# Product ends by eight k tiles and token halves, and two modulation rows moved beside the indexer, in a two-block transformer kernel

## The chip, the core and the metric

The kernel runs on one core of a Trainium2 chip. The metric is the time of one execution on the device in microseconds. The engines named below are TensorE (PE, matrix products), VectorE (DVE), ScalarE (ACT), GpSimd (POOL) and SyncE (SP), which only issues loads here.

## What is computed

256 tokens of width 1024 go through two transformer blocks of different make, all in float32. Cut to the products and the modulation:

```python
# block 1
h = h + rms_norm(nsa_gmlp_mixer(rms_norm(h)) @ w_out)          # w_out 1024x1024
gate, up = split(rms_norm(h) @ w_gate_up)                      # 1024 x 2*2816
h = h + rms_norm((silu(gate) * up) @ w_down)                   # 2816x1024
# block 2
mod = (silu(c) @ ada_w + ada_b)                                # 1024 x 6*1024
shift_m, scale_m, gate_m, shift_f, scale_f, gate_f = split(mod)   # rows 0 to 5
h = rmsnorm(x) * (1 + scale_m) + shift_m
q_lat, kv_lat, k_idx, w_idx, z, xbc, dt_raw, g_a, g_b = split(h @ w_in)
y_a = sparse_mla_attention(...)    # indexer scores -> top 64 keys -> attention
y_b = ssd_mixer(z, xbc, dt_raw, ...)
x = x + gate_m * rmsnorm((sigmoid(g_a) * (y_a @ w_o_attn) + sigmoid(g_b) * (y_b @ w_o_ssd)) @ w_out)
h2 = rmsnorm(x) * (1 + scale_f) + shift_f
u_gate, u_up = split(h2 @ w_ffn_in)
x = x + gate_f * rmsnorm((silu(u_gate) * u_up) @ w_ffn_out)
```

## The kernel before

**Products.** The 256 tokens are two halves t of 128. Every float32 operand is held as two parts, hi and lo, and a product is three matmuls: hi x hi, lo x hi, hi x lo (`mm3`, L285 to L287; L362 to L364 in `projT`, which makes the transposed result with 256 columns). Weights come in raw tiles of 512 KB that SP loads (`wload`, L268) into NRAW = 6 buffers; ACT copies each to hi (L277) and DVE subtracts to get lo (L278), into NHI = 4 pairs. A raw buffer is free again when its lo is made, a pair when its last matmul has read it.

**proj2** makes a product with 1024 output columns: four k tiles at a time, first half t = 0, then t = 1, two PSUM tiles of 512 columns each (named ma for t = 0 and mb for t = 1). When a half is done, `residual` takes it through a norm, adds it to x, norms again, transposes (`transpose_split`, PE tile tr, L256) and splits the result to xT, which the next product reads. DVE's steps of this chain are L374 to L394, the split of the transposes L245.

**ffn** takes the gate columns 0 to 511 for both halves (PSUM ma), then the up columns (mb), then the remaining columns, then w_down by proj2.

**Work woven in.** `weave` takes steps of two generators by given costs (SCHED). Beside the first feed-forward run `adas` and `key_bias`. `adas((2, 4, 3))` makes three rows of mod: for each row eight loads araw with own buffers, eight accumulations on DVE (L575 the first, L577 the others), and a sum over partitions by four matmuls on 32 columns at a time (L583). `key_bias` has eight steps: a load rb (L683), issued one step ahead into two buffers, two DVE instructions (L696, L697), 48 matmuls (L703), copies by ACT (L705), and four stores of 1 MB (kb) from ACT's queue. Row 5 is made beside the second feed-forward. Rows 1 and 0 are made by a third form, `adas_pe` (L544), before the stages treated here.

**The indexer stage.** `indexer()` makes qi, then for each t eight idx steps: four matmuls (L1210) into a PSUM tile, ACT's Relu (L1213), two DVE accumulations (L1219); then the top-k of the half (L1229, L1230). `weave` sets it beside zproj (the last z columns, `projT`), `steps` (softplus and running sums, L1109 to L1126), four products `gproj` and ssd_in. Engines work through their instructions in the order in which the program issues them, so this order is the schedule.

## Time and profile before

| | us |
|---|---|
| median of 3 runs (lowest, highest) | 1005.57 (999.85, 1005.75) |
| profiled execution | 1006.56 |
| its span, first to last instruction | 1004.8 |
| PE busy | 938.7 (93%) |
| DVE busy | 719.2 (72%) |
| ACT busy | 509.0 (51%) |
| POOL busy | 35.9 (4%) |

200.01 MB are moved, 199 GB/s on the mean; TensorE's mean granted clock is 0.969 of full speed. PE counts as busy when a matmul is under way, also a slow one. The stages are, in the span's microseconds: w_out to 175.2, the first feed-forward to about 392, the indexer stage from about 418 to 580, w_out_2 782 to 807, the second feed-forward to 1002.

### The profile page before, as it was taken

Reading aid. Unit: us, or ns where it says so; the run is one execution under the profiler, and the core shown is the slowest. Engines: PE = TensorE matmul, PEld = TensorE weight load, DVE = VectorE, ACT = ScalarE, POOL = GpSimd, SP = SyncE. Lnnn points to the kernel's source line nnn. Section 1 sums busy time; section 2 is a strip of 40 time slices with the busy share of each in tenths; the row PEclk is TensorE's granted clock in tenths of the full one; section 3 lists DMA queues with packets and bytes.
Section 4 is the critical chain, followed back from the end, with each engine's and each line's share of the span. In section 5 each row is a group of like instructions: output and inputs, shape, how many; then the busy total and the mean of one; then the engine's idle time right before and its main releaser. Section 6 shows DMA issues by size and latency. Waiting matters only on the chain.

```text
span 1004.8 us, 16187 instructions
## 1 busy us (share of the span) xinstructions
PE 938.7 (93%) x6161; PEld 790.0 (79%) x6161; DVE 719.2 (72%) x1305; ACT 509.0 (51%) x873; POOL 35.9 (4%) x63
## 2 busy tenths in 40 slices
PE   8879988899999997899799999999999979999997
PEld 6755656689998775797688789899867859999885
DVE  5754864697978577579988657899876677776544
ACT  5333634453445335465557656867753454544432
POOL 2000001000000001100000000000000010000000
PEclk9997998999999999899989999999999999999999
DMA  9775557888899894565444179677665668766651
GB/s 296 210 250 205 169 168 205 256 222 273 224 300 288 271 299 123 136 179 160 147 128 152 57 225 235 168 176 205 179 178 169 208 180 269 233 199 182 226 171 42
DMA packets 157115, 200.01 MB, mean 199 GB/s; under 512 B 14868, under 2 KB 118317, under 8 KB 157037
## 3 DMA queue, kind: packets, MB, share of 16 engines
q1 hardware_dynamic: 137840, 184.61, 61.6%
q10 hardware_dynamic: 16268, 8.30, 3.0%
q0 software_dynamic: 2928, 6.07, 2.0%
q8 instruction: 48, 0.79, 0.3%
q14 instruction: 31, 0.25, 0.1%
HBM read 193.39 MB, written 5.54 MB: 198 GB/s over the span
## 4 chain that ended last, share of the span: by engine, by line
PE 68%; DMA 13%; DVE 10%; issue 3%; ACT 3%; POOL 1%; SPq 0%; ACTq 0%; DVEq 0%; POOLq 0%
PE ma L286 7%; PE ma L287 7%; PE ma L285 7%; DMA raw<-in_w_gate_up_dram 5%; PE ma L362 4%; PE ma L364 4%; PE ma L363 4%; PE mb L286 4%; PE mb L287 4%; PE mb L285 4%; PE mb L362 4%; PE mb L363 3%; PE mb L364 3%; DVE lo L278 3%; DMA rb<-t 2%
## 5 line engine op out<-in xcount | busy, mean ns | idle before, releaser
L278 DVE TENSOR_TENSOR lo<-raw,hi 128x1024 fp32r<-128x1024 f32 (+2 forms) x266 | 320.7, 1213 | 133.5 <-ACT hi L277 129.2
L277 ACT CAST hi<-raw 128x1024 fp32r<-128x1024 f32 (+2 forms) x266 | 275.4, 1044 | 255.4 <-PE mb L287 78.8
L364 PE MATMUL ma<-xTh,lo 128*128 128x256 f32 x512 | 144.7, 283 | 6.8 <-DVE lo L278 6.8
L362 PE MATMUL ma<-xTh,hi 128*128 128x256 f32 x512 | 146.5, 286 | 1.0 <-ACT hi L277 1.0
L363 PE MATMUL ma<-xTl,hi 128*128 128x256 f32 x512 | 144.3, 282 | 0.0
L362 PE MATMUL mb<-xTh,hi 128*128 128x256 f32 x384 | 106.9, 278 | 0.0
L363 PE MATMUL mb<-xTl,hi 128*128 128x256 f32 x384 | 106.6, 278 | 0.0
L364 PE MATMUL mb<-xTh,lo 128*128 128x256 f32 x384 | 106.5, 277 | 0.0
L364 PEld LDWEIGHTS ma<-xTh,lo 128*128 128x128 f32 x512 | 98.3, 192 | 8.0 <-DVE lo L278 7.6
L362 PEld LDWEIGHTS ma<-xTh,hi 128*128 128x128 f32 x512 | 98.3, 192 | 4.1 <-issue 2.5
L363 PEld LDWEIGHTS ma<-xTl,hi 128*128 128x128 f32 x512 | 98.2, 192 | 1.0 <-issue 0.8
L286 PE MATMUL ma<-lo,xTh 128*128 128x512 f32 (+2 forms) x208 | 84.4, 407 | 11.3 <-DVE lo L278 11.3
L285 PE MATMUL ma<-hi,xTh 128*128 128x512 f32 (+2 forms) x208 | 84.2, 408 | 0.1
L287 PE MATMUL ma<-hi,xTl 128*128 128x512 f32 (+2 forms) x208 | 83.8, 403 | 0.2
L362 PEld LDWEIGHTS mb<-xTh,hi 128*128 128x128 f32 x384 | 72.2, 188 | 1.2 <-issue 1.2
L363 PEld LDWEIGHTS mb<-xTl,hi 128*128 128x128 f32 x384 | 72.2, 188 | 0.8 <-issue 0.8
L364 PEld LDWEIGHTS mb<-xTh,lo 128*128 128x128 f32 x384 | 72.2, 188 | 0.6 <-DVE lo L278 0.4
L286 PEld LDWEIGHTS ma<-lo,xTh 128*128 128x128 f32 x208 | 41.3, 198 | 22.4 <-DVE lo L278 14.3
L285 PEld LDWEIGHTS ma<-hi,xTh 128*128 128x128 f32 x208 | 40.7, 197 | 12.0 <-issue 2.9
L287 PEld LDWEIGHTS ma<-hi,xTl 128*128 128x128 f32 x208 | 41.0, 197 | 9.1 <-DVE xTl L245 1.1
L286 PE MATMUL ma<-lo,hTh 128*128 128x512 f32 x88 | 35.4, 402 | 4.4 <-DVE lo L278 4.4
L577 DVE SCALAR_TENSOR_TENSOR ada<-araw,t,ada 128x1024 f32<-128x1024 f32 x28 | 35.8, 1279 | 5.0 <-DMA araw<-in_ada_w_dram 5.0
(431 smaller groups left out, 1805.2 us busy)
## 6 DMA issues: line engine op xcount, KB each, us to landing
raw<-in_w_in_dram SPq DMA_DIRECT2D x80, 512.0 KB, 4.7
raw<-in_w_gate_up_dram SPq DMA_DIRECT2D x44, 512.0 KB, 11.7
raw<-in_w_ffn_in_dram SPq DMA_DIRECT2D x44, 512.0 KB, 4.7
araw<-in_ada_w_dram SPq DMA_DIRECT2D x32, 512.0 KB, 5.6
raw<-in_w_down_dram SPq DMA_DIRECT2D x22, 512.0 KB, 10.7
raw<-in_w_ffn_out_dram SPq DMA_DIRECT2D x22, 512.0 KB, 3.5
raw<-in_w_out_dram SPq DMA_DIRECT2D x16, 512.0 KB, 4.4
cw<-in_ada_w_dram SPq DMA_DIRECT2D x16, 512.0 KB, 4.0
```

The costliest lines, as they stand in the source:

```text
L277: s.copy(hi, raw)
L278: v.tensor_tensor(lo, raw, hi.bitcast(F32), op=OP.subtract)
L285: pe.matmul(out, xh, wh, start=start, stop=False)
L286: pe.matmul(out, xh, wl, start=False, stop=False)
L287: pe.matmul(out, xl, wh, start=False, stop=stop)
L362: pe.matmul(out, hi[:, k % pc, fs], xh[:, k], start=k == 0, stop=False)
L363: pe.matmul(out, hi[:, k % pc, fs], xl[:, k], start=False, stop=False)
L364: pe.matmul(out, lo[:, k % pc, fs], xh[:, k], start=False, stop=k == KT - 1)
L577: v.scalar_tensor_tensor(acc, raw, cc, acc, op0=OP.mult, op1=OP.add)
```

## The change

It has three parts. (1) For w_out and w_out_2 `proj2` takes `tail=8`: the last group has all eight k tiles (w_down and w_ffn_out keep four), so that t = 0 is done with 48 matmuls of t = 1 still to come. Of the eight, the first four go k tile by k tile, the last four by column half. Four more pairs hx and lx (pool tx) are used in turn with hi and lo, from the product to the first four steps of the feed-forward behind it. (2) The feed-forward's first gate and up products are taken in turn by half: gate and up of t = 0, then of t = 1; four steps of this are taken before `weave` starts. (3) Rows 4 and 3 leave `adas`; `ada_fill` makes them in steps driven by the indexer: 16 loads into the common raw buffers, and for each 128x1024 tile four matmuls (L607 after) that sum over k in PSUM, with one DVE addition a row. `key_bias` goes ahead of `adas` in their mix.

```diff
-SCHED = {"a1": (2.0, 1.08), "f1": (3.0, 3.8), "f1ada": (2, 4, 3), "a2": (2.0, 0.63), "f2": (3.0, 1.45),
+SCHED = {"a1": (2.0, 1.08), "f1": (3.0, 3.1), "f1ada": (2,), "a2": (2.0, 0.63), "f2": (3.0, 1.45),
...
+    def deeper(side=None):
+        with pool("tx", side="right") as tx:
+            deep[:] = [tx, -1]
...
     def wsplit(raw, shape):
         n = int(np.prod(shape))
-        hi = T(wp, [P, CH], F32R, tag="hi", bufs=NHI)[:, :n].rearrange("p (a n) -> p a n", a=shape[0])
-        lo = T(wp, [P, CH], F32R, tag="lo", bufs=NHI)[:, :n].rearrange("p (a n) -> p a n", a=shape[0])
+        pl, tags, bufs = wp, ("hi", "lo"), NHI
+        if deep:
+            deep[1] = (deep[1] + 1) % (NHI + NTX)
+            if deep[1] >= NHI:
+                pl, tags, bufs = deep[0], ("hx", "lx"), NTX
+        hi, lo = (T(pl, [P, CH], F32R, tag=z, bufs=bufs)[:, :n].rearrange("p (a n) -> p a n", a=shape[0])
+                  for z in tags)
...
-                for ci, c in [(ci, c) for c in range(2) for ci in grp] if last else [(ci, c) for ci in grp for c in range(2)]:
+                cut = max(0, len(grp) - 4) if last else len(grp)
+                for ci, c in [(ci, c) for ci in grp[:cut] for c in range(2)] + [(ci, c) for c in range(2)
+                                                                               for ci in grp[cut:]]:
...
-            yield from proj(w_up, 0, 512, 8, xT, keep, sizes=(4,))
-            yield from proj(w_up, DFF, 512, 8, xT, finish(0, 512), sizes=(4,), bank=mb)
+            yield from mix(proj(w_up, 0, 512, 8, xT, keep, sizes=(4,)),
+                           proj(w_up, DFF, 512, 8, xT, finish(0, 512), sizes=(4,), bank=mb))
...
+    def ada_fill(js):
...
+                raws[i] = wload(ktile(I["ada_w_2"], k, 1, j * D, D), (1, 1024))[:, 0]
+        load(0)
+        load(1)
+        yield
+        for i, (j, k) in enumerate(todo):
+            raw = raws.pop(i)
+            if k == 0:
+                b = mb()[:, :256]
+            for c in range(4):
+                pe.matmul(b[c * 32:(c + 1) * 32], c32[:, k], raw[:, c * 256:(c + 1) * 256], start=k == 0, stop=k == 7)
+            load(i + 2)
+            if k == 7:
+                q = qs[j]
+                v.tensor_tensor(q[:, 0], b, q[:, 0], op=OP.add)
+                mod_store(j, q[:, 0], q[:, 1] if j in gains else None)
+            yield
...
-        run(proj2(I["w_out"][0], 8, mT, ev_o, order=[4, 5, 6, 7, 0, 1, 2, 3]))
+        run(proj2(I["w_out"][0], 8, mT, ev_o, order=[4, 5, 6, 7, 0, 1, 2, 3], tail=8))
...
-    weave((ffn(xT, I["w_gate_up"][0], I["w_down"][0], rf, ev_f1), wa),
-          (mix(adas(SCHED["f1ada"], rp), key_bias()), wd))
+    with pool("rp", side="right") as rp:
+        weave((f1g, wa), (mix(key_bias(), adas(SCHED["f1ada"], rp)), wd))
...
-    weave((seq(indexer(), latent_v(), heads()), wa), (seq(zproj(NZ0, NZ - NZ0), once(steps, srow), *gproj, ssd_in(0, ap)), wf))
+    weave((seq(indexer(ada_fill((4, 3))), latent_v(), heads()), wa),
+          (seq(zproj(NZ0, NZ - NZ0), once(steps, srow), *gproj, ssd_in(0, ap)), wf))
...
-    shift = mod_row(3, sp, "E0", 2)
+    shift = T(bp, [P, 2, 1024], tag="mixp")[:, 0]
+    g.dma_start(shift, bass.AP(tensor=mods[3, :].tensor, offset=mods[3, :].offset, ap=[[0, P], [1, D]]))
```

The change moves instructions. On PE, where w_out ends and the gate product of the first feed-forward begins (xTh and xTl are the product's input, hi, lo, hx and lx the weights, ma and mb its PSUM tiles, tr the transposes of the second half), before:

```order
L286 MATMUL ma_1714<-lo_1719,xTh_1463 128x512
L287 MATMUL ma_1714<-hi_1718,xTl_1464 128x512
L285 MATMUL ma_1714<-hi_1724,xTh_1463 128x512
L256 MATMUL tr_1678<-t_74,scr_1661 128x128 x4
L256 MATMUL tr_1690<-t_74,scr_1662 128x128 x4
L285 MATMUL ma_1715<-hi_1718,xTh_1463 128x512
L286 MATMUL ma_1715<-lo_1719,xTh_1463 128x512
L286 MATMUL ma_1714<-lo_1725,xTh_1463 128x512
```

and after, 24 gate and six up matmuls behind the product's end:

```order
L311 MATMUL mb_1765<-hx_1769,xTl_1470 128x512
L309 MATMUL mb_1765<-hx_1769,xTh_1469 128x512
L310 MATMUL mb_1765<-lx_1770,xTh_1469 128x512
L311 MATMUL mb_1765<-hx_1769,xTl_1470 128x512
L262 MATMUL tr_1684<-t_74,scr_1667 128x128 x4
L262 MATMUL tr_1696<-t_74,scr_1668 128x128 x4
L309 MATMUL mb_1765<-hx_1775,xTh_1469 128x512
L310 MATMUL mb_1765<-lx_1776,xTh_1469 128x512
```

The transposes of t = 1 stood behind seven gate matmuls and stand behind 30 matmuls of t = 0.

On SP in the second half of w_down (raw tiles and the loads rb and araw), before:

```order
L268 DMA raw_3634<-in_w_down_dram 128x1024
L268 DMA raw_3640<-in_w_down_dram 128x1024
L268 DMA araw_3382<-in_ada_w_dram 128x1024
L268 DMA raw_3676<-in_w_down_dram 128x1024
L268 DMA araw_3517<-in_ada_w_dram 128x1024
L268 DMA raw_3682<-in_w_down_dram 128x1024
L268 DMA araw_3538<-in_ada_w_dram 128x1024
L683 DMA rb_672_3521<-t_113 128x1x2048
L268 DMA araw_3605<-in_ada_w_dram 128x1024
L268 DMA raw_3745<-in_w_down_dram 128x1024
```

and after:

```order
L274 DMA raw_3501<-in_w_down_dram 128x1024
L746 DMA rb_639_3297<-t_114 128x1x2048
L274 DMA raw_3588<-in_w_down_dram 128x1024
L274 DMA raw_3594<-in_w_down_dram 128x1024
L274 DMA raw_3654<-in_w_down_dram 128x1024
L274 DMA raw_3660<-in_w_down_dram 128x1024
L746 DMA rb_649_3402<-t_114 128x1x2048
L274 DMA raw_3717<-in_w_down_dram 128x1024
L274 DMA raw_3723<-in_w_down_dram 128x1024
L274 DMA raw_3753<-in_w_down_dram 128x1024
L746 DMA rb_665_3519<-t_114 128x1x2048
```

The araw loads are gone; the distance between rb loads is nine loads before, and four and three after.

On PE at the first idx steps (at, with mTh or mTl), with ma of gproj, and in the changed kernel mb of ada_fill, before:

```order
L1210 MATMUL at_4614<-t_4073,mTl_4389 128x256
L1210 MATMUL at_4614<-t_4074,mTl_4389 128x256
L1210 MATMUL at_4614<-t_4073,mTl_4389 128x256
L1210 MATMUL at_4614<-t_4074,mTl_4389 128x256
L285 MATMUL ma_4702<-hi_4706,xTh_3941 128x512
L286 MATMUL ma_4702<-lo_4707,xTh_3941 128x512
L287 MATMUL ma_4702<-hi_4706,xTl_3942 128x512
L285 MATMUL ma_4702<-hi_4706,xTh_3941 128x512
```

and after:

```order
L1279 MATMUL at_4581<-t_4009,mTh_4324 128x256
L1279 MATMUL at_4581<-t_4008,mTh_4324 128x256
L1279 MATMUL at_4581<-t_4009,mTh_4324 128x256
L607 MATMUL mb_4559<-raw_4564,ada_4540 32x256 x4
L607 MATMUL mb_4559<-raw_4579,ada_4540 32x256 x4
L607 MATMUL mb_4559<-raw_4594,ada_4540 32x256 x4
L607 MATMUL mb_4559<-raw_4652,ada_4540 32x256 x4
L607 MATMUL mb_4559<-raw_4667,ada_4540 32x256 x4
L607 MATMUL mb_4559<-raw_4682,ada_4540 32x256 x4
L309 MATMUL ma_4684<-hi_4688,xTh_3877 128x512
L309 MATMUL ma_4685<-hi_4688,xTh_3877 128x512
```

gproj's first matmuls stood behind the second idx step; now the third idx step and eight tiles of ada_fill stand ahead of them.

On SP, the loads of the same place, before:

```order
L268 DMA raw_4497<-in_w_qidx_dram 128x2x512
L268 DMA raw_4537<-in_w_in_dram 128x8x128
L268 DMA raw_4568<-in_w_in_dram 128x8x128
L268 DMA raw_4704<-in_w_in_dram 128x2x512
L268 DMA raw_4710<-in_w_in_dram 128x2x512
L268 DMA raw_4787<-in_w_in_dram 128x2x512
```

and after:

```order
L274 DMA raw_4594<-in_ada_w_dram 128x1024
L274 DMA raw_4652<-in_ada_w_dram 128x1024
L274 DMA raw_4667<-in_ada_w_dram 128x1024
L274 DMA raw_4682<-in_ada_w_dram 128x1024
L274 DMA raw_4686<-in_w_in_dram 128x2x512
L274 DMA raw_4692<-in_w_in_dram 128x2x512
L274 DMA raw_4723<-in_ada_w_dram 128x1024
L274 DMA raw_4738<-in_ada_w_dram 128x1024
```

gproj's first two loads (raw_4686 and raw_4692) stand behind eight loads of ada_w in the same six buffers.

## Rows read from the trace of the kernel before

**Rows 1.** Busy time of each engine by stretch, with TensorE's clock and DMA.
```profile
core 0: us, PE busy (x) PEld busy (x) DVE busy (x) ACT busy (x) POOL busy (x), PEclk, DMA share, GB/s
175.22:204.90 29.68, 25.99 (x109) 20.22 (x108) 20.97 (x29) 15.01 (x21) 2.46 (x4) 0.94 0.73 227
226.00:372.00 146.00, 139.31 (x1229) 126.08 (x1228) 111.05 (x121) 61.04 (x73) 3.28 (x5) 0.99 0.89 274
478.00:510.00 32.00, 25.85 (x165) 24.00 (x165) 31.29 (x88) 13.94 (x23) 0.00 (x0) 0.89 0.49 146
510.00:568.00 58.00, 56.84 (x358) 45.05 (x357) 49.08 (x148) 40.37 (x104) 0.00 (x0) 1.00 0.41 128
800.00:825.00 25.00, 19.07 (x80) 14.64 (x79) 18.61 (x29) 12.96 (x25) 4.52 (x6) 0.93 0.49 145
850.00:925.00 75.00, 75.00 (x665) 74.46 (x664) 52.63 (x56) 36.25 (x41) 0.57 (x1) 1.00 0.69 215
```

**Rows 2.** Timeline of PE, end of w_out: start, duration, line, tiles, idle before.
```profile
176.52 0.39 PE L287 MATMUL ma<-hi,xTl 128*128 128x512 f32 x1
176.75 0.40 PE L285 MATMUL ma<-hi,xTh 128*128 128x512 f32 x1
179.81 1.67 PE L256 MATMUL tr<-t,scr 128*128 128x128 f32 x8 [2.67 <-DVE scr L388]
...
182.99 0.63 PE L285 MATMUL ma<-hi,xTh 128*128 128x512 f32 x1
183.41 0.60 PE L286 MATMUL ma<-lo,xTh 128*128 128x512 f32 x1
```

**Rows 3.** The page's DMA issues: count, KB each, median us to landing.
```profile
raw<-in_w_in_dram SPq DMA_DIRECT2D x80, 512.0 KB, 4.7
raw<-in_w_gate_up_dram SPq DMA_DIRECT2D x44, 512.0 KB, 11.7
raw<-in_w_ffn_in_dram SPq DMA_DIRECT2D x44, 512.0 KB, 4.7
```

**Rows 4.** Timeline of PE, start of the second feed-forward.
```profile
814.20 0.50 PE L286 MATMUL ma<-lo,xTh 128*128 128x512 f32 x1 [3.79 <-DVE lo L278]
815.49 1.94 PE L256 MATMUL tr<-t,scr 128*128 128x128 f32 x8 [0.78 <-DVE scr L394]
```

**Rows 5.** Timeline of DVE in the same stretch.
```profile
806.52 0.69 DVE L374 TENSOR_TENSOR scr<-mb,row 128x512 f32<-128x512 f32 x1
...
814.59 1.41 DVE L394 SCALAR_TENSOR_TENSOR scr<-scr,rx,E 128x512 f32<-128x512 f32 x2 [0.44 <-POOL rx L220]
```

**Rows 6.** The page's costliest groups: busy, mean ns, idle before them.
```profile
L278 DVE TENSOR_TENSOR lo<-raw,hi 128x1024 fp32r<-128x1024 f32 (+2 forms) x266 | 320.7, 1213 | 133.5 <-ACT hi L277 129.2
```

**Rows 7.** Groups of instructions by line, 200 to 372 us.
```profile
L577 DVE SCALAR_TENSOR_TENSOR ada<-araw,t,ada 128x1024 f32<-128x1024 f32 x21 | 26.9, 1279 | 5.0 <-DMA araw<-in_ada_w_dram 5.0
```

**Rows 8.** Timeline of PE, first feed-forward.
```profile
249.90 0.64 PE L583 MATMUL at<-ada,t 128*32 128x256 f32 x8
```

**Rows 9.** Timeline of all engines in w_down.
```profile
350.40 0.81 DVE L696 TENSOR_SCALAR oh<-rb,t 128x2048 bf16<-128x2048 bf16 x1 [6.48 <-DMA rb<-t]
...
353.66 0.19 PEld L286 LDWEIGHTS ma<-lo,hTh 128*128 128x128 f32 x1 [3.04 <-DVE lo L278]
```

**Rows 10.** Instructions of the tile rb on SP: first and last start.
```profile
L683 SPq DMA_DIRECT2D rb<-t x8: 537/542/1252, 163.6 to 331.9; - x8
```

**Rows 11.** DMA issues, 158 to 372 us.
```profile
t<-kb ACTq DMA_DIRECT2D x4, 1024.0 KB, 20.3
```

**Rows 12.** Timeline of PE, first idx steps and first gproj product.
```profile
450.26 0.40 PE L285 MATMUL ma<-hi,xTh 128*128 128x512 f32 x1
...
452.06 0.75 PE L1210 MATMUL at<-t,mTh 128*128 128x256 f32 x4 [0.24 <-ACT bq L1213]
```

**Rows 13.** Timeline of DVE, end of the softplus chain.
```profile
466.85 0.49 DVE L1117 TENSOR_TENSOR scr<-scr,t 128x128 f32<-128x128 f32 x2
```

**Rows 14.** Timeline of PE behind the indexer's top-k.
```profile
502.26 0.58 PE L364 MATMUL ma<-xTh,lo 128*128 128x256 f32 x1 [6.15 <-DVE lo L278]
```

More of the change, by code (lines that the diff above doesn't have):

```diff
@@ L36 @@
 NHI = 4
+NTX = 4
 NSCR = 3
@@ L167, in mix, with take @@
                     live.remove(gn)
+    def take(gen, n):
+        for _ in range(n):
+            next(gen)
+            yield
     def mark(engines=QUEUED):
@@ L478, in ffn @@
                 yield from projT(w_up, DFF + f0 * P, 2 * P, 8, xT, finishT(f0), mb)
-            yield from proj2(w_down, 22, hT, evac)
+            yield from proj2(w_down, 22, hT, evac, tail=4)
     def gelu2(out, a, sq_scale, th_scale):
@@ L551, in adas_pe, with load @@
                 mod_store(j, q[:, 0], q[:, 1] if j in gains else None)
+    def ada_fill(js):
+        yield
+        buf = T(per, [P, 1024], tag="ada", bufs=1)
+        qs, o = {}, 0
+        for j in js:
+            n = 2 if j in gains else 1
+            qs[j] = buf[:, o * 256:(o + n) * 256].rearrange("p (a n) -> p a n", a=n)
+            mod_quarters(j, qs[j])
+            o += n
+        c32 = buf[:, 768:].rearrange("p (k n) -> p k n", k=8)
+        v.tensor_copy(c32, c8[:, :, None].to_broadcast([P, 8, 32]))
+        todo = [(j, k) for j in js for k in range(8)]
+        raws = {}
+        def load(i):
+            if i < len(todo):
+                j, k = todo[i]
+                raws[i] = wload(ktile(I["ada_w_2"], k, 1, j * D, D), (1, 1024))[:, 0]
+        load(0)
+        load(1)
+        yield
+        for i, (j, k) in enumerate(todo):
[9 more added lines that the diff above has]
+                mod_store(j, q[:, 0], q[:, 1] if j in gains else None)
+            yield
     def adas(js, pl):
@@ L709, in key_bias @@
                 yield
-    with pool("a1") as ap, pool("a1w") as aw:
+    with pool("a1") as ap:
+        awg = pool("a1w")
+        aw = awg.__enter__()
         W = I["w_in"][0]
@@ L1010, in body @@
                        gm_fin(0), gm_fin(1)), wf))
+        awg.__exit__(None, None, None)
+        pqg.__exit__(None, None, None)
+        txg = deeper()
+        txg.__enter__()
         prow = row(I["norm_mix_post"], D, eng=g)
@@ L1033, in ev_f1 @@
         residual(t, accs, prow, mrow["g"], mrow["s"], xT2[0], False)
+    f1g = ffn(xT, I["w_gate_up"][0], I["w_down"][0], rf, ev_f1)
+    run(take(f1g, 4))
+    txg.__exit__(None, None, None)
     wa, wd = SCHED["f1"]
-    weave((ffn(xT, I["w_gate_up"][0], I["w_down"][0], rf, ev_f1), wa),
-          (mix(adas(SCHED["f1ada"], rp), key_bias()), wd))
-    rpg.__exit__(None, None, None)
-    ppg.__exit__(None, None, None)
+    with pool("rp", side="right") as rp:
+        weave((f1g, wa), (mix(key_bias(), adas(SCHED["f1ada"], rp)), wd))
     xT = xT2[0]
@@ L1044, in body @@
     bp = b2g.__enter__()
-    mixp = T(bp, [P, 2, 1024])
+    mixp = T(bp, [P, 2, 1024], tag="mixp")
     yz = [T(bp, [P, 2, S], tag="yz", bufs=5) for _ in range(4)]
@@ L1189, in ev_lat, with indexer @@
         split_ps(b[:, 384:512], kiT[0][:, sl], kiT[1][:, sl])
-    def indexer():
+    def indexer(other):
+        next(other)
         qi = pair(ap, 8, "mT")
@@ L1202, in indexer @@
         yield from projT(I["w_qidx_2"], 0, 1024, 2, qnT, ev_qi, mb)
+        next(other)
         for t in range(2):
@@ L1219, in indexer @@
                         v.scalar_tensor_tensor(acc, r[:, i * S:(i + 1) * S], w, acc, op0=OP.mult, op1=OP.add)
+                next(other)
                 yield
@@ L1431, in ev_yb @@
         if not mxT:
-            mxT["h"] = [T(sp, [P, 4, S], F32R, tag=tag) for tag in ("bc", "xs")]
+            mxT["h"] = [T(mx, [P, 4, S], F32R, tag="mxh", bufs=2) for _ in range(2)]
             mxT["l"] = [T(bp, [P, 4, S], F32R, tag="b0", bufs=2) for _ in range(2)]
@@ L1455, in ev_o2 @@
         residual(t, accs, gq, scale, shift, xT, False)
-    run(proj2(I["w_out_2"], 8, lambda k: (mxT["h"][k // 4][:, k % 4], mxT["l"][k // 4][:, k % 4]), ev_o2))
-    spg.__exit__(None, None, None)
+    run(proj2(I["w_out_2"], 8, lambda k: (mxT["h"][k // 4][:, k % 4], mxT["l"][k // 4][:, k % 4]), ev_o2,
+              tail=8))
     b2g.__exit__(None, None, None)
@@ L1469, in ev_f @@
             eng.dma_start(O["out"][0, t * P:(t + 1) * P, cs], x[:, t, cs])
+    f2g = ffn(xT, I["w_ffn_in_2"], I["w_ffn_out_2"], None, ev_f)
+    run(take(f2g, 4))
+    txg.__exit__(None, None, None)
+    mxg.__exit__(None, None, None)
     with pool("f2", side="right") as fp2:
         wa, wd = SCHED["f2"]
-        weave((ffn(xT, I["w_ffn_in_2"], I["w_ffn_out_2"], None, ev_f), wa),
-              (adas(SCHED["f2ada"], fp2), wd))
+        weave((f2g, wa), (adas(SCHED["f2ada"], fp2), wd))
     ctx.close()
```

17 lines of the change are left out of this document (14 added, 3 removed).

## The prediction

> **What bounds the kernel now.** I read the busy shares first, then the table by stage, then the timeline of the stages that are not full. TensorE (PE) is the bound. Where nothing disturbs it, it is full: in the second feed-forward it is busy 75.00 of 75 us at clock 1.00 [rows 1]. So a gain can only come from stretches where PE stands or runs at a lower granted clock, and the table names them: the start of the first feed-forward (25.99 busy of 29.68, clock 0.94), the rest of it (139.31 of 146), the indexer's end (25.85 of 32, clock 0.89) and the start of the second feed-forward (19.07 of 25, clock 0.93). In the indexer's end VectorE (DVE) is busy 31.29 of 32 us, so DVE is the bound there, and PE behind it again (56.84 of 58) [rows 1].
>
> The change touches all four. Below, each gets the microseconds that can be won or lost. The sum is made against the profiled execution, 1006.56 us, which is 1.0 over the median of the runs, 1005.57.
>
> **Place 1, w_out to the first gate and up products.** A 512-column matmul starts 0.23 us after the last one at full clock (176.52, 176.75 [rows 2]). Seven matmuls after the product's end PE stops for 2.67 us, because the transposes of the second token half stand next in its order and their input L388 is not ready; behind them the spacing is 0.43 us (182.99 to 183.41 [rows 2]), the lower of the clock's two levels (1.2 of 2.4 GHz). The stage holds 97 such matmuls and 12 transposes; eight of these took 1.67 us at the lower level [rows 2], so 0.1 each at the full one. 97 x 0.23 + 12 x 0.1 = 23.5 us; it took 29.68 [rows 1], so 6.2 us are lost: the wait, some 2 us of low clock, and the rest in short waits for splits. After the change 24 gate and 6 up matmuls of the first half, 30 x 0.23 = 6.9 us, stand ahead of those transposes, and the chain that they wait for ended 4.6 us after 175.2. The wait is covered with 2 us to spare, and with it goes the low clock behind it. What is late next: the up tiles of this half are needed 24 matmuls after the start, 5.5 us, where before they had 11. They are eight loads in six buffers; the first splits no longer wait for w_out's buffers, since four more pairs are there, and the araw and rb loads that shared the queue now come behind twelve gate and up loads. Those loads took 11.7 us to land, against 4.7 for the same shape in the second feed-forward [rows 3]. At 4.7 they are in time, at 11.7 some 3 us would be lost again. Bounds -2 and -6.2; nothing is added on PE. I take **-5**, near the end of the 4.7 because the two kinds of loads that made the queue long are behind.
>
> **Place 2, w_out_2 to the second feed-forward.** Here DVE is the chain. PE's two long waits are 3.79 and 0.78 us [rows 4], and in 800 to 825 it stands for 5.9 us in all at clock 0.93 [rows 1]; the 0.07 x 25 = 1.8 us of the clock, and another 1.5 of matmuls and transposes that lie apart, make about 9. DVE is at its chain from the second half's first product (806.52) to its last step L394 (814.59 + 1.41) [rows 5], with two splits of 1.2 us [rows 6] and the first half's remainder in between. Taking all eight k tiles in one group puts 48 matmuls, not 24, between the first half's end and the second's: 24 x 0.23 = 5.5 us more cover for the first half's chain, whose transposes now come before the end of the product. Then 24 gate and 9 up matmuls (7.6 us) stand ahead of the second half's transposes; the second half's chain takes 806.5 to 815.5, 9 us, and carries about two splits fewer of the first half but four of its own, so 1.5 to 2.5 us stay. The first pass of the product has a price: it needs a k tile per 6 x 0.23 = 1.4 us while DVE makes a split in 1.2 us [rows 6], no slack for anything else; I put 1 us on that, and its low-clock echo another 1. So 9 - 4 = **-5**, bounds -2 (the DVE chain stays the bound) and -8 (only the 1.5 stays). The shift row goes into mixp's buffer and is loaded by POOL behind mixp's last reader; the product's first 48 matmuls, 11 us, hide that load, and if they don't it costs what is left of its landing, 2 us at most by the loads of this size [rows 3].
>
> **Rows 4 and 3 out of the first feed-forward.** What goes: 16 loads of 512 KB, 8.4 MB, 16 of DVE's steps of 1.28 us [rows 7], 20.5 us at most (the first of a row is shorter), and two blocks L583 of eight narrow matmuls, 0.64 us each [rows 8]. In 226 to 372 PE stands for 6.7 of 146 us, and DMA moves 274 GB/s at a share of 0.89 [rows 1]. DVE itself is at 111 of 146, so its own time is not the price; the price is its order. Its splits come late because it stood 5.0 us at L577 for ada loads [rows 7] and 6.48 us at L696 for an rb load; that one ended at 350.40, and PE got its split 2.62 us late at 353.66 [rows 9]. The waits for ada go for certain where no row is left. The rb load was issued at 331.9 [rows 10], one step of key_bias ahead, and landed 18.4 us later; what counts is whether it lands within one step's matmuls. Before, two rb loads stood among those of w_down; the change packs four there, and w_down is 22 x 12 matmuls, 264 x 0.23 = 61 us, so a step is some 15 us, of which DVE takes 2 for its own. In this stretch 40 MB were moved (274 GB/s x 146 us), and 8.4 of them leave: at 79% of 18.4 the landing is 14.5 us, level with the step. PE's 6.7 us of standing, 1.3 of blocks and 0.01 x 146 = 1.5 of low clock make 9.5 at most; if rb waits as before, the gain is 3; if three or four of the steps wait, it is 0. I take **-6**, the middle of the upper half, since the landing comes out level.
> The Trainium skill (DMA: Bandwidth & Descriptors, Queues, rings and completion order) says that each DMA engine serves the rows of queues that hold work in turn, packet by packet; by that, the stores of kb on ScalarE's queue, 20.3 us each [rows 11], would take turns with the loads whether or not the ada loads are there, and the gain here would be the 3, the sum -9.
>
> **The same two rows beside the indexer.** What comes: 16 loads into the six common raw buffers, and 64 matmuls 128x256 on 32 columns. No row shows four in a group; eight at L583 took 0.64 us between wide matmuls [rows 8], so four cost 0.33 to 0.64, and 16 groups 5.3 to 10.2 us. I take 5.3. The loads matter more. In the order of PE six groups in a row stand ahead of the first gproj product, which started at 450.26 before [rows 12]; that product's weights go into buffers that the third and fourth of these groups release, at about 452.4, since they stand behind the third idx step (452.06 [rows 12]). A w_in load lands in 4.7 us [rows 3], and its copy on ScalarE stands before the first matmul, about as long as the split of the same size, 1.2 us [rows 6]: gproj starts near 458.5. Of the six us two are filled by the groups, so PE stands about 4 to 6 and restarts slowly. Queued behind on PE: all of gproj and the idx steps; those have to wait for DVE's softplus chain until 467 anyway (L1117 at 466.85 [rows 13]). So PE is delayed by about 5.3 + 6 = 11.3 us. It gets part back: PE stood for 6.15 us before 502.26 [rows 14] and then ran slowly, 32 - 25.85 = 6.15 idle and (1 - 0.89) x 32 = 3.5 by the clock [rows 1], because DVE had the mask to make; the deferred gproj matmuls fill just that. Full cover gives 11.3 - 9.6 = 1.7, none gives 11.3; below zero is excluded but for 1 us of noise, since nothing is removed here. I take **+4**: nearer the cover, because the idx steps that start DVE's chain are not moved by PE, and not all of it, because gproj's remaining splits come to DVE later too.
> The Trainium skill (TensorEngine Tiling (Array Packing), Key Properties) says that a change of tile mode drains TensorE; the groups make 11 blocks, 22 changes. With the 128 cycles that the Trainium skill gives for a drain (TensorE: Matmul & The Clock Gate, What happens when you issue a matmul) that is an estimate of 1.2 us, and the sum would be -10.8. The block of eight in [rows 8] holds two changes in its 0.64 us already, so I add nothing.
>
> **Sum:** -5 - 5 - 6 + 4 = -12: 1006.6 becomes 994.6, and less the 1.0 to the median **994 us**.
>
> **Rivals.**
> *The hole in the indexer is carried through* (11.3, not 4). For it: PE is busy 56.84 of 58 us behind it, so nothing later takes up a delay, and DVE at 31.29 of 32 may shift as a whole. Against: the idle time that gproj can fill. Sum -4.7: 1001.
> *rb keeps ffn1 waiting* (0 to -3). For it: the packed loads and the 20.3 us stores. Against: a fifth of the stretch's bytes leave the queue. Sum -6 to -9: 997 to 1000.
> *The halves do not do what they say* at place 2: DVE's chain is the bound with any order of PE, gain there -2. Sum -9: 997.
> *Slower:* the ada tiles lock the six raw buffers. From the point where each of the four gproj pairs and the uq load waits for a matmul that itself waits for its landing, each costs 4.7 + 1.2 and a place in the queue, about 7 us, 5 x 7 = 35 less the 9.6 us of idle time, so +25: -16 + 25 = +9, with the slow restarts (2 us each) +18: 1015 to 1024. Against: pairs two and three are issued well ahead in the order of SP.
>
> **How the numbers follow.** A measurement of this kernel tells about 1% from no change, 995.5 to 1015.6. Chances: the forecast 0.45 (988 to 999); indexer carried through 0.18; rb waits 0.12; halves without effect 0.07; two of these together 0.05 (1001 to 1007); everything at its good end (-6.2 - 8 - 9.5 + 1.7, 984) 0.05; slower 0.08. Faster by over 1%: 0.31 of the forecast's 0.45, the good end, and 0.12 of the single rivals at their lower ends, 0.48. Slower by over 1%: 0.08 less what of it stays below 1015.6, 0.06. Same: 0.46. Range: the outer bounds leave out the good end and the slower case and some of the doubles, **985 to 1005**.
>
> **What would show it.** Place 1: no transposes with an idle time ahead of them after the product's end, clock 1.00 in the 30 us behind it. Place 2: the first half's transposes ahead of the product's last matmul; one wait of 1 to 3 us in place of the two. ffn1: L577 gone behind the first row; one or two waits at L696 left, under 5 us together. Indexer: PE idle 4 to 6 us between the idx steps and gproj near 452 to 459, and the idle time before 502 gone or shorter. The prediction is wrong if that hole is over 10 us or comes again at the second gproj pair, or if PE waits for DMA at the first up tiles.

## The result and the profile after

The changed kernel takes 1013.66 us (median of 7 runs, 1010.05 to 1015.71) where the kernel before takes 1003.37 on the same chips: ratio 1.0105, 95% interval 1.0072 to 1.0139. It is slower by 1%, where 994 was forecast. Its profiled execution has a span of 1013.9 us against 1004.8, so the two traces can be compared piece by piece.

The pieces are taken between starts of the same matmul in both traces: the last one of w_out, the last one of w_down, the first idx step, the first one of w_out_2 and the first one of w_ffn_out.

| piece | before | after | difference | forecast |
|---|---|---|---|---|
| first feed-forward (places 1 and rows) | 216.5 | 226.5 | +10.0 | -11 |
| to the first idx step | 57.8 | 58.8 | +1.0 | 0 |
| first idx step to w_out_2 | 333.4 | 339.8 | +6.4 | +4 |
| w_out_2 to w_ffn_out | 155.1 | 146.9 | -8.2 | -5 |

These sum to +9.2; the spans differ by 9.1. Of the three pieces with a forecast other than 0 two came out with its sign; the first feed-forward is 21 us off. Between the first and the last matmul of w_down the time went from 74.8 to 87.0 us, in the part ahead of it from 141.7 to 139.5, so the loss lies in w_down.

The table by stage, after (columns as in [rows 1]; the last two stretches are moved by 10 and 17 us to the same work):

```profile
core 0: us, PE busy (x) PEld busy (x) DVE busy (x) ACT busy (x) POOL busy (x), PEclk, DMA share, GB/s
174.98:204.66 29.68, 29.68 (x139) 24.17 (x138) 18.77 (x30) 14.24 (x23) 5.06 (x8) 1.00 0.75 214
226.00:372.00 146.00, 131.75 (x1199) 121.16 (x1199) 93.70 (x106) 59.48 (x71) 2.60 (x4) 0.95 0.74 207
320.00:375.00 55.00, 41.20 (x318) 33.35 (x314) 20.23 (x19) 15.71 (x19) 0.00 (x0) 0.88 0.61 172
488.00:520.00 32.00, 31.43 (x187) 23.29 (x187) 31.37 (x79) 18.15 (x28) 0.58 (x1) 1.00 0.98 302
817.00:842.00 25.00, 24.15 (x115) 19.02 (x114) 22.11 (x30) 14.13 (x24) 4.90 (x5) 1.00 0.60 182
```

The first 29.68 us behind w_out are now full: PE 29.68, clock 1.00, against 25.99 and 0.94 in [rows 1], and 139 matmuls in place of 109. The end of w_out_2 with the start of the second feed-forward has 24.15 of 25 busy, against 19.07. But 226 to 372 holds 131.75 busy where it held 139.31, at clock 0.95, and in 320 to 375 PE works 41.20 of 55 us at clock 0.88. DMA is not the reason by its load: its share in 226 to 372 fell from 0.89 to 0.74.

**Place 1** itself went as forecast. The timeline of PE at the second half's transposes, after:

```profile
181.32 0.39 PE L310 MATMUL mb<-lx,xTh 128*128 128x512 f32 x1
181.55 0.40 PE L311 MATMUL mb<-hx,xTl 128*128 128x512 f32 x1
181.81 1.23 PE L262 MATMUL tr<-t,scr 128*128 128x128 f32 x8
182.79 0.48 PE L309 MATMUL mb<-hx,xTh 128*128 128x512 f32 x1
183.11 0.39 PE L310 MATMUL mb<-lx,xTh 128*128 128x512 f32 x1
183.33 0.40 PE L311 MATMUL mb<-hx,xTl 128*128 128x512 f32 x1
```

They start without an idle time ahead (2.67 us in [rows 2]) and the 512-column matmuls around them keep the spacing of 0.22 to 0.23 us.

**What took it back.** The timeline of PE 30 us later, and of SP ahead of it (SP's rows: start, time from the first to the last issue, count):

```profile
209.63 0.40 PE L311 MATMUL ma<-hi,xTl 128*128 128x512 f32 x1
213.38 0.87 PE L766 MATMUL at<-t,rb 128*128 128x64 bf16 x24 [3.35 <-DVE rb L760]
...
215.50 0.80 PE L310 MATMUL mb<-lo,xTh 128*128 128x512 f32 x1 [0.94 <-DVE lo L302]
216.09 0.63 PE L311 MATMUL mb<-hi,xTl 128*128 128x512 f32 x1
216.52 0.63 PE L309 MATMUL mb<-hi,xTh 128*128 128x512 f32 x1
```

```profile
160.14 36.28 SPq L274 DMA_DIRECT2D raw<-in_w_gate_up_dram  x16
196.47 0.68 SPq L746 DMA_DIRECT2D rb<-t  x1
197.25 1.72 SPq L274 DMA_DIRECT2D araw<-in_ada_w_dram  x2
199.02 0.55 SPq L746 DMA_DIRECT2D rb<-t  x1
199.63 18.50 SPq L274 DMA_DIRECT2D araw<-in_ada_w_dram  x3
218.22 6.94 SPq L274 DMA_DIRECT2D raw<-in_w_gate_up_dram  x5
```

PE stands 3.35 us for the first rb tile and then 0.94 for a split, and the matmuls behind it are spaced 0.43 us until 221, the clock's lower level: 3.4 + 0.9 + about 12 x 0.2 us, some 7, about the whole gain of place 1. The first rb load left at 196.47 where it left at 163.6 before [rows 10]: in the program's order it stands behind 16 gate and up loads (the prediction had twelve), and its pool takes the place of the extra pairs. Behind it SP stood 18.5 us over three araw loads, and the next gate and up loads left at 218.22.

**w_down.** What PE and DVE waited for in 160 to 400, and DVE's three last waits for rb with the issues of these loads on SP:

```profile
PE at L766 <- DVE rb L760: 13.9, 4, 6.9
```

```profile
DVE oh L759 <- DMA rb<-t: 40.4, 4, 10.5
```

```profile
326.94 0.81 DVE L759 TENSOR_SCALAR oh<-rb,t 128x2048 bf16<-128x2048 bf16 x1 [10.20 <-DMA rb<-t]
...
346.14 0.81 DVE L759 TENSOR_SCALAR oh<-rb,t 128x2048 bf16<-128x2048 bf16 x1 [10.51 <-DMA rb<-t]
...
360.41 0.81 DVE L759 TENSOR_SCALAR oh<-rb,t 128x2048 bf16<-128x2048 bf16 x1 [9.93 <-DMA rb<-t]
```

```profile
314.34 0.54 SPq L746 DMA_DIRECT2D rb<-t  x1
...
332.41 0.54 SPq L746 DMA_DIRECT2D rb<-t  x1
...
349.75 0.54 SPq L746 DMA_DIRECT2D rb<-t  x1
```

Before, DVE waited once for rb, 6.48 us [rows 9], and PE not for more than 1.1 us. Now DVE waits four times, 40.4 us, and the splits of w_down stand behind. DVE has these loads 12.6, 13.7 and 10.7 us after their issue, sooner than the 18.4 of before, and it did not help: each is issued when the matmuls of the step before have freed its buffer, and DVE comes to it 0.7 to 3.2 us later.

**Place 2**, PE at the transposes, before and after:

```profile
806.08 0.63 PE L256 MATMUL tr<-t,scr 128*128 128x128 f32 x4 [0.76 <-DVE scr L394]
806.47 0.48 PE L287 MATMUL mb<-hi,b 128*128 128x512 f32 x1
```

```profile
821.65 0.63 PE L262 MATMUL tr<-t,scr 128*128 128x128 f32 x4 [0.60 <-DVE scr L420]
...
823.96 0.40 PE L311 MATMUL mb<-hx,b 128*128 128x512 f32 x1
...
832.19 0.63 PE L262 MATMUL tr<-t,scr 128*128 128x128 f32 x4 [0.25 <-DVE scr L420]
```

The first half's transposes start 2.3 us ahead of the product's last matmul (821.65 and 823.96), before the change 0.4 us ahead of it (806.08 and 806.47). PE's waits in this place are 0.60 us for them and 0.25 for the second half's (832.19), 0.8 in all, where they were 5.8 in all before, with 3.79 and 0.78 of [rows 4] among them.

**The indexer**, PE at the first idx steps:

```profile
459.91 0.63 PE L1279 MATMUL at<-t,mTh 128*128 128x256 f32 x4
460.46 0.64 PE L607 MATMUL mb<-raw,ada 128*32 128x256 f32 x8
461.03 0.74 PE L1279 MATMUL at<-t,mTl 128*128 128x256 f32 x4
...
462.95 1.93 PE L607 MATMUL mb<-raw,ada 128*32 128x256 f32 x32
465.06 0.64 PE L607 MATMUL mb<-raw,ada 128*32 128x256 f32 x8 [0.17 <-DMA raw<-in_ada_w_dram]
466.83 0.64 PE L607 MATMUL mb<-raw,ada 128*32 128x256 f32 x8 [1.14 <-DMA raw<-in_ada_w_dram]
469.56 0.74 PE L309 MATMUL ma<-hi,xTh 128*128 128x512 f32 x2 [2.09 <-ACT hi L301]
```

The hole ahead of gproj is 1.1 + 2.1 + 0.6 us and a slow restart, what was forecast, and the wait of 6.15 us behind the top-k [rows 14] is gone. What was not: the matmuls of the rows themselves. In the trace they are 128 instructions, two for each of the 64 in the program:

```profile
459.90:799.70 339.80, 9.60 (x128) 2.82 (x128) 0.98 0.68 190
```

9.6 us of PE, where 5.3 were put, at the low end of the prediction's 5.3 to 10.2.

### The profile page after: what moved, and what is told of

Read it like the earlier page. It is cut to its first block, busy times and chain, and to the rows that moved or that the text cites. A ratio compares the mean times of both kernels' runs of the same rounds, so it can differ in the third digit from the quotient of the medians.

```text
span 1013.9 us, 16375 instructions
## 1 busy us (share of the span) xinstructions
PE 947.0 (93%) x6273; PEld 794.7 (78%) x6273; DVE 702.8 (69%) x1290; ACT 508.9 (50%) x873; POOL 36.9 (4%) x63
## 4 chain that ended last, share of the span: by engine, by line
PE 75%; DMA 11%; DVE 7%; issue 2%; ACT 2%; POOL 1%; SPq 1%; ACTq 0%; DVEq 0%; POOLq 0%
PE ma L310 7%; PE ma L309 6%; PE ma L311 6%; PE ma L388 5%; PE ma L389 5%; PE ma L390 5%; PE mb L388 5%; PE mb L390 5%; PE mb L389 4%; PE mb L310 4%; PE mb L309 4%; PE mb L311 4%; DMA rb<-t 4%; DVE lo L302 2%; DMA araw<-in_ada_w_dram 2%
## 5 line engine op out<-in xcount | busy, mean ns | idle before, releaser
L302 DVE TENSOR_TENSOR lo<-raw,hi 128x1024 fp32r<-128x1024 f32 (+2 forms) x250 | 301.4, 1213 | 128.7 <-ACT hi L301 124.0
L301 ACT CAST hi<-raw 128x1024 fp32r<-128x1024 f32 (+2 forms) x250 | 259.4, 1043 | 246.6 <-PE mb L311 91.3
L309 PE MATMUL ma<-hi,hTh 128*128 128x512 f32 x88 | 35.8, 411 | 0.0
```

The source lines that it names most:

```text
L301: s.copy(hi, raw)
L302: v.tensor_tensor(lo, raw, hi.bitcast(F32), op=OP.subtract)
L309: pe.matmul(out, xh, wh, start=start, stop=False)
```

## The experiments

All are compared with the kernel before in runs on the same chip. The last three columns are the first feed-forward, the first idx step to w_out_2, and w_out_2 to w_ffn_out, from the profiled execution of each.

| run | median us | ratio (95%) | ffn1 | indexer on | place 2 |
|---|---|---|---|---|---|
| before (profile) | 1003 to 1006 | 1 | 216.5 | 333.4 | 155.1 |
| after | 1013.66 | 1.0105 (1.0072 to 1.0139) | 226.5 | 339.8 | 146.9 |
| x1_halves_only | 1002.22 | 0.9974 (0.9936 to 1.0012) | 218.4 | 327.1 | 147.0 |
| x2_rows_only | 1015.19 | 1.0119 (1.0059 to 1.0178) | 213.2 | 343.2 | 158.2 |
| x3_rb_ahead | 1008.43 | 1.0047 (1.0021 to 1.0074) | 221.1 | 339.1 | 146.9 |
| x5_halves_rb_ahead | 994.98 | 0.9929 (0.9894 to 0.9965) | 219.0 | 329.2 | 147.4 |
| x6_halves_rb_early | 988.42 | 0.9847 (0.9803 to 0.9890) | 216.5 | 335.5 | 147.4 |
| x10_rb_spread | 1012.16 | 1.0083 (1.0049 to 1.0116) | 226.3 | 340.8 | 147.0 |
| x8_no_ada_loads | 1011.52 (one) | | 222.0 | 339.6 | 147.5 |
| x9_no_ada_matmuls | 1009.54 (one) | | 222.2 | 337.9 | 146.9 |
| x11_rb_parts | 988.79 | 0.9862 (0.9790 to 0.9934) | 201.3 | 339.3 | 146.9 |
| x12_halves_early_parts | 978.65 | 0.9766 (0.9715 to 0.9818) | 205.1 | 328.5 | 147.5 |
| x13_before_parts | 994.53 | 0.9914 (0.9883 to 0.9945) | 206.6 | 329.9 | 158.2 |
| x14_rows_early_parts | 989.95 | 0.9882 (0.9825 to 0.9938) | 200.9 | 336.9 | 146.9 |
| x15_rb_columns | 1007.23 | 1.0006 (0.9966 to 1.0046) | 220.4 | 340.6 | 147.6 |
| x16_halves_parts | 987.72 | 0.9826 (0.9762 to 0.9890) | 208.2 | 328.7 | 147.5 |

The column from the first idx step to w_out_2 scatters by some 4 us among runs whose stage is the same, so single differences below that say nothing. A profiled execution need not lie at the median either: that of x1 is the shortest of its ten, 8 us under their median, those of x5, x6, x10 and x13 lie 3, 7, 6 and 5 us over theirs.

**Theory and rivals.** Theory: the loss of the first feed-forward is rb, late and slow, in front of DVE's splits. Rivals: the halves with their extra pairs starve w_down; the rows cost it all beside the indexer.

**The two parts apart.** x1 puts the rows back:

```diff
-"f1": (3.0, 3.1), "f1ada": (2,)
+"f1": (3.0, 3.8), "f1ada": (2, 4, 3)
-mix(key_bias(), adas(SCHED["f1ada"], rp))
+mix(adas(SCHED["f1ada"], rp), key_bias())
-indexer(ada_fill((4, 3)))
+indexer(repeat(None))
```

> The two rows stay in the first feed-forward with the old cost and order of the mix; the product ends by eight k tiles, the extra pairs and the halves stay. Theory (the rows are what costs: rb loads one step ahead in a w_down without ada steps, +10 us, and the indexer, +7): both go, the two places keep -7 and -8; rb's first load, still behind twelve gate and up loads, may take back up to 7. Some 988 to 996 us where before is 1003.4, ratio 0.985 to 0.993; PE's waits for rb in w_down as before (one, under 3 us). Rival (the halves themselves delay rb and the splits of w_down): the +10 in w_down stays, 998 to 1003.

x2 leaves the rows moved and undoes tail=8, the extra pairs and the order by halves:

> The two rows beside the indexer and the new cost of the mix as in the changed kernel; product ends, halves and extra pairs as before. Theory: w_down loses 10 us to rb, the indexer 7, nothing is won: 1018 to 1023 us, ratio 1.015 to 1.02. Rival (the loss needs the halves): 1000 to 1008.

x1 measured 1002.22, over the theory's 988 to 996 and within the rival's 998 to 1003; place 2 keeps its 8 us, and even in this execution the first feed-forward is 2 us longer than before. The longest waits of PE there:

```profile
PE at L768 <- DVE rb L762: 9.6, 2, 8.4
```

8.4 us of the 9.6 are the first rb tile, issued at 194.6. So in the first feed-forward the halves alone win nothing. x2 measured 1015.19, under the 1018 expected: in its profile the first feed-forward is 3.3 us shorter and the indexer's stage 9.8 longer, with w_down at 74.3 us. So the rows do not lose in w_down by themselves, as the theory had it, and that part of it fell. In the profiles it looks as if both parts were needed: w_down takes 74.8 us before, 76.6 in x1, 74.3 in x2, and 87.0 after (83 to 88 in the four runs that change only rb's source, its cut by columns or the ada tiles). The ratios do not bear that out: -0.3% for x1 and +1.2% for x2 add up to +0.9%, both together measured +1.05%. Where x1's longer executions lose time was not profiled, so a joint effect of the two parts is not shown.

**rb deeper and earlier.** x3 (rows moved) and x5 (rows in place) have a third buffer:

```diff
-NRB = 2
+NRB = 3
...
         load(0)
+        load(1)
...
-            load(n + 1)
+            load(n + 2)
...
-            oh = T(rp, [P, 8, S], BF, tag="oh", bufs=1)
+            oh = scr().bitcast(BF).rearrange("p (a n) -> p a n", a=8)
```

> The changed kernel with a third rb buffer, loads two steps ahead instead of one; oh lies in a scr buffer to make room. Theory (the loop of rb, buffer free - load 11 to 14 us - DVE 2 us - matmuls, is longer than a step of 15 us): DVE's 40 us of waits for rb fall under 8, PE's 14 us under 3, w_down wins 10 to 15: 999 to 1005 us. Rival (the queue is too full for rb in any order, or the splits of w_down are short of DVE time): waits stay above 20 us, 1010 to 1015.

> As the halves-only run, with the third rb buffer and loads two steps ahead. Theory: 2 to 6 us under the halves-only run, since its one wait for rb at w_down and the one at the first step get shorter: 984 to 992. Rival (ada loads in the same queue are the bound there): the same as the halves-only run within 1.5 us.

x3 measured 1008.43, over the 999 to 1005 expected. It wins 5 us in the first feed-forward and not the 10 to 15: DVE's waits for rb fall from 40.4 to 9.8 us, but ACT then stands 18.5 us for a store of kb, and PE 7.3 us behind it. x5 is 7 us under x1, 994.98 where 984 to 992 were expected; where the 7 us lie can't be read from the two profiles, of which one is its kernel's shortest and the other its longest. The first rb tile still holds PE for 9.7 us. x6 is x5 with the first loads ahead of the gate loads, in a pool of their own:

```diff
+        rbg = pool("rbp", side="right")
+        rbp = rbg.__enter__()
         txg = deeper()
...
+    kbg = key_bias()
+    run(take(kbg, 1))
     f1g = ffn(xT, I["w_gate_up"][0], I["w_down"][0], rf, ev_f1)
```

> As the run with halves and rb two steps ahead, but the first three rb loads stand ahead of the first gate and up loads, in buffers of their own pool. Theory (in all runs with halves the gain of the first place is given back near 210 us because rb's first load, at 194 to 199 behind the 16 gate and up loads, lands after its matmuls' turn, and SP stands behind it at an araw load): PE's wait at the first rb matmuls (8 to 13 us) goes, 984 to 990 us, ratio 0.982 to 0.988. Rival (the araw loads alone hold SP and PE there): within 2 us of the run without, 993 to 997.

988.42, as the theory had it, 7 under x5. The two profiled executions are only 3 us apart: 2.5 less in the first feed-forward, 6.6 less from there to the first idx step (53.0 against 59.6), and 6.3 more behind it. PE's wait at the first rb tile is gone; of the 5.0 us that are left for rb 4.6 are one wait in w_down.

**Why rb lands slowly.** x10 reads other rows of DRAM, so that its bias is another one:

```diff
-offset=rd.offset + n * 32 * S, ap=[[8 * S, 4], [0, 32], [1, 8 * S]]
+offset=rd.offset, ap=[[0, 4], [8 * S, 32], [1, 8 * S]]
```

> The changed kernel, each rb load of the same 512 KB, but from 32 different rows of DRAM, each read 4 times, in place of 4 rows, each read 32 times; the bias of block 1 is then another one. Theory A (a load that reads the same 4 KB row 32 times lands slowly by itself): landing falls from 11 to 14 us to 5 to 7, DVE's 40 us of waits for rb fall under 10, 1000 to 1006 us. Theory B (the landing is set by what else is in the queues and by 128 rows of 4 KB): landing within 2 us of before, 1011 to 1015.

Nothing moves; the landings in w_down stay at 11.5 to 13.3 us and DVE's waits at

```profile
DVE oh L759 <- DMA rb<-t: 41.1, 4, 11.2
```

So it is not the row that is read 32 times. The view of the DMA in the last landing of the changed kernel shows another thing (share of the 16 engines in tenths over 40 slices, and GB/s):

```profile
DMA  0037887994547998778823221222212322321110
GB/s 0 0 121 243 334 334 288 379 273 137 182 167 228 334 319 167 167 182 167 167 61 76 61 76 76 106 76 91 106 61 91 121 76 91 121 106 76 76 61 30
```

For the last 5 us only two tenths of the engines work, about 4 of 16, at 60 to 120 GB/s; they carry rb and the rest of the one weight load issued behind it. The trace also keeps when a load raises its semaphore. Each of the three rb loads does so five times, once 1 us after its issue and four times at its end: the one issued at 314.34 at 315.3 and at 326.4 to 326.9. The weight load issued behind it at 315.00 does so 16 times, twelve times by 322.1 and four times at 327.7 to 328.3. Read as one raise an engine, four engines are late, with rb and with the weights queued behind it. The Trainium skill (DMA: Bandwidth & Descriptors, Why a DMA increments its semaphore by 16 and not by 1) says that a load runs on the largest number of engines up to 16 that divides the slowest dimension of both its sides. The trace agrees: rb's source has a slowest dimension of 4 rows. x11 writes it as four loads of 32 partitions, on the changed kernel, x13 on the kernel before:

```diff
-                sy.dma_start(rbs[n], ... ap=[[8 * S, 4], [0, 32], [1, 8 * S]])
+                for r in range(4):
+                    sy.dma_start(rbs[n][32 * r:32 * r + 32], bass.AP(tensor=rd.tensor,
+                        offset=rd.offset + (n * 32 + r * 8) * S, ap=[[0, 32], [1, 8 * S]]))
```

> The changed kernel, each rb load written as four loads of 32 partitions. Theory (in the last 4 to 7 us of each rb landing only 0.2 of the DMA engines are busy at 60 to 120 GB/s: the load, whose slowest dimension is 4 rows, runs on 4 of 16 engines; in parts of 32 x 4 KB it uses all): landing falls from 11 to 14 us to 5 to 8, DVE's waits for rb from 40 to under 15 us, w_down's 10 us go: 1000 to 1006 us, ratio 0.995 to 1.002. Rival (landing is the queue ahead of rb, not its own engines): 1009 to 1015.

> The kernel before with rb in four parts and nothing else. Theory: the one wait of 6.5 us of DVE for rb goes and the queue is shorter for raw: 2 to 6 us faster, ratio 0.994 to 0.998. Rival (before, the loads stand behind ada and raw loads): no change, 0.998 to 1.002.

x11: 988.79, 25 us under the changed kernel, more than the theory had. DMA at its first such load in w_down, and PE in the stretch of w_down:

```profile
DMA  9999999998998999989999999999999999999898
DMA packets 3983, 3.34 MB, mean 372 GB/s; under 512 B 107, under 2 KB 3607, under 8 KB 3982
```

```profile
320.00:375.00 55.00, 54.39 (x365) 44.21 (x363) 28.65 (x30) 25.46 (x35) 1.11 (x2) 1.00 0.71 217
```

The engines are busy to nine tenths at 372 GB/s, DVE's waits that end with an rb load are one of 2.8 us, and PE is busy 54.39 of 55 us at clock 1.00, against 41.20 at 0.88. Every part raises its semaphore 16 times, and the weight load issued at 321.95, behind one step's parts, has all its 16 at 325.1 to 326.0. x13 shows that the kernel before paid for it too: 9 us where 2 to 6 were expected. It paid with more than DVE's wait of 6.48 us. ACT's waits for weight loads in the first feed-forward, before and in x13:

```profile
ACT hi L277 <- DMA raw<-in_w_gate_up_dram: 17.4, 7, 4.9
ACT hi L277 <- DMA raw<-in_w_down_dram: 14.6, 4, 6.6
```

```profile
ACT hi L277 <- DMA raw<-in_w_gate_up_dram: 5.9, 3, 4.8
```

The other reading, that four small loads slip between the raw loads, is tried by x15: four loads that keep the slowest dimension of 4.

```diff
+                for r in range(4):
+                    sy.dma_start(rbs[n][:, 2 * r:2 * r + 2], bass.AP(tensor=rd.tensor,
+                        offset=rd.offset + n * 32 * S + r * 2 * S, ap=[[8 * S, 4], [0, 32], [1, 2 * S]]))
```

> The changed kernel, each rb load as four loads, but of 128 partitions and a quarter of the columns, so that the slowest dimension stays 4 rows. Theory (4 of 16 engines): nothing is won, the share of DMA engines stays near 0.2 at the end of each landing, DVE waits over 30 us for rb, 1009 to 1018 us. Rival (four smaller loads are what helps): as the run in parts of 32 partitions, 985 to 993.

```profile
DVE oh L760 <- DMA rb<-t: 37.1, 4, 10.0
```

```profile
DMA  2220000029588322992269998998222222200786
```

The waits stay, and so do the two tenths. The window holds one step: its parts are issued from 343.38 and landed at 353.9, 10.5 us later, and from 346 to 353 their packets, 1 KB in this run, keep about four engines busy (3.8 to 4.5). The stretches of 2s at both ends are the rest of the weight loads behind such a step, on the last four engines. Of the 24 us that x11 wins by the ratios (1.0105 to 0.9862) x15 wins 10 (1.0006), of the 25 in the first feed-forward 6: 1007.23, a little under the 1009 to 1018 expected. What four loads win by themselves was not looked into; the engines give the rest.

**The rows beside the indexer.** x8 reads a resident tile in place of the loads, x9 keeps the loads and makes 16 of the 64 matmuls:

```diff
-                raws[i] = wload(ktile(I["ada_w_2"], k, 1, j * D, D), (1, 1024))[:, 0]
+                raws[i] = x[:, 0]
```

```diff
+                if k in (0, 7):
                     pe.matmul(b[c * 32:(c + 1) * 32], c32[:, k], raw[:, c * 256:(c + 1) * 256], ...)
```

> The changed kernel without the 16 ada loads beside the indexer: the 64 matmuls read a resident tile instead, so rows 4 and 3 have other values. It splits the 7.7 us that the stage lost. If the loads in the six raw buffers cost (gproj's weights wait for ada tiles), the stage from the first idx step to w_o_attn comes within 2 to 3 us of before; if the matmuls and their tile changes cost, it stays 6 to 8 us longer.

> The changed kernel with the 16 ada loads but with the matmuls of the first and last tile of each row only (16 of 64), so rows 4 and 3 have other values. If the loads cost, the stage stays 5 to 8 us longer than before; if the matmuls cost, 2 to 3.

339.6 and 337.9 against 339.8 with both: neither brings the stage back to the 333.4 of before, and both differences lie within the scatter. Over all runs it is 340.0 on the mean with the rows there (after, x2, x3, x10, x11, x14, x15, 336.9 to 343.2) and 330.3 without (before, x1, x5, x6, x12, x13, x16 and their 327.1 to 335.5). That is some 10 us for the move. PE's own time for the 64 matmuls is 9.6, but x9 took 7.2 of it away (three quarters) and won 1.9, so that this time alone is not the cost, nor are the loads alone. In the profiles PE is busy 321.4 us in this stage before and 330.7 after and stands 12.0 and 9.2; in x9 it is busy 324.7 and stands 13.2, 4.3 of it in one wait for a split. So the 9.2 us that the move adds to PE's work hide 2.8 us of its waits, and most of what x9 takes away comes back as waits. What sets the stage's length then, and whether the new order of PE costs without either, stays open.

**Together.** x12 has the halves, the third buffer, the early loads and the parts, with the rows in the first feed-forward; x14 the same with the rows beside the indexer; x16 the halves and the parts alone.

> Halves, rows in the first feed-forward, third rb buffer, early rb loads, and rb in four parts. Theory: the waits for rb (5 us of PE) and part of those for araw go on top of the run without parts, 982 to 987 us. Rival (with two steps ahead the landing no longer matters): the same as that run, 987 to 991.

> The changed kernel with the two rows beside the indexer, third rb buffer, early rb loads and rb in four parts: the same as the halves run with these, but for the place of the rows. Theory (the rows cost 8 us beside the indexer and win about 5 in a first feed-forward that no longer waits for rb): 985 to 991, 2 to 5 us above the run with the rows left in place. Rival (with rb out of the way the rows win more than they cost): equal or faster than it.

> Halves and extra pairs, rows left in the first feed-forward, rb in four parts of 32 partitions, two rb buffers, no early loads. Theory (once rb lands in half the time its depth and its place matter little): within 3 us of the run with all of these, 977 to 982. Rival (the first rb loads at 194, behind 15 gate and up loads, still come too late): 983 to 988.

x12 is the fastest, 978.65, 2.3% under the kernel before and under the 982 to 987 of the theory. PE's waits for rb in the first feed-forward are 0.4 us there. With rb in parts the halves win on the kernel before what they did not win in x1: the ratio is 0.9826 in x16 and 0.9914 in x13.

x14 is 11 us over it, where 2 to 5 were expected: the rows win 4 us in the first feed-forward and cost 6 between it and the first idx step (59.8 against 53.5 us) and 8 behind. x16 is 9 over it, 6 by the ratios, whose intervals overlap; it lies in the rival's range, so that the third buffer and the early loads seem still worth something. In the profiles only 3 of the 9 lie in the first feed-forward; 6 lie behind it, up to the first idx step (59.6 against 53.5), where PE waits 5.1 us for the norm of w_down's second half in x16 and 0.4 in x12. The two edits were not tried apart with the parts; without them x5 and x6 differ by the early loads alone, and there the same wait goes from 4.2 to 0.4 us.

## Why the prediction was wrong

**Place 1** (-5): the mechanism and the size were right, and more, 30 matmuls, 6.9 us, in the first 29.68 us; the whole part ahead of w_down came out only 2.2 us shorter. What failed is the sentence that the araw and rb loads, put behind the gate and up loads, free the queue for these. It named the queue that they left and not who waits for them: rb's first tile has a fixed place in DVE's and PE's order, and PE is there 14 us after the load's issue and stands 3.35 us. x6 shows the place by moving the rb loads alone.

**Rows out of the first feed-forward** (-6, bounds 0 and -9.5): the step that failed is the one on the rb load. It let a wait begin only where the landing is longer than a step of 15 us. The load leaves when the matmuls of the step before free the buffer, and DVE's turn for it comes at once, ahead of the splits; with rows gone from the mix there are fewer instructions between two turns. So the bound of 0 at the bad end had no ground: the packed steps were named in the prediction and a loss was not allowed for. w_down came out 12.2 us longer, with 40.4 us of DVE's waits for rb in the first feed-forward. The landing itself came out under the 14.5 us that the prediction had (10.7 to 13.7), but not for its reason, the bytes in the queue: the queue was only 0.6 to 0.74 full, and x11 against x15 shows that the four engines set it. The prediction also put the late split of [rows 9] to DVE's wait for rb alone; ACT stood 6.62 us for a weight load in the same place, until 352.72, and x13 shows that this was rb's price too. The wait for ada loads, which was to go, did go (5.0 to 0.2 us), and without the halves the first feed-forward is 3.3 us shorter (x2).

**Halves and rows together**: in the profiles each alone leaves the first feed-forward within 3.3 us of before (x1 +1.9, x2 -3.3) and both give +10, which neither term held. By the ratios the two add up, so that this stays open.

**Place 2** (-5): -8.2, just beyond the good bound of -8; x2 and x13, which keep the old order there, took 158.2 us and not 155.1, so that it may be more. The 1.5 to 2.5 us that were to stay of the second half's chain came out as 0.25, and the two microseconds put on the product's first pass and its echo were not seen.

**The indexer** (+4, between 1.7 and 11.3): +6.4, and some 10 over all runs. The hole (4 to 6 us) and the idle time given back (6.15) were right. The term that was mis-sized is PE's time: [rows 8] show x8 for a block of four matmuls of the program, since the trace counts each float32 matmul of this form twice, and the prediction took it as eight. Sixteen blocks at 0.6 are 9.6 us, not 5.3. Read rightly the term would have been +8; that is near what was measured, but x9 does not bear out that it is PE's time that sets it. The sentence on tile modes is borne out: 16 matmuls in one run took 1.94 us (462.95 to 465.06 less 0.17 of wait) and four with a change on either side 0.57 (460.46 to 461.03), so four times this is 0.34 more, 0.11 for each change pair. The Trainium skill (TensorEngine Tiling (Array Packing), Key Properties) says that a change of tile mode drains TensorE. With the 128 cycles that the Trainium skill gives for a drain (TensorE: Matmul & The Clock Gate, What happens when you issue a matmul) two drains are an estimate of 0.11 us; the trace agrees.

The rival that came true is the second, with a sign that it was not given. The slower rival, raw buffers locked by ada tiles, did not happen: PE waited 1.3 us for those loads. In its sum five slow restarts of 2 us make +19, not +18; nothing else rests on it.
